# The first branch's output projection as seven products of split halves, with the gate weights in half rows beside it

## The chip, the cores and the metric

One core of one Trainium2 chip runs the whole kernel in one launch. The metric is device time in microseconds (us), as the median over executions.

## The reference

One decoder layer over 2048 tokens with 1024 channels, then a final RMSNorm:

```python
mod = c @ w_ada + b_ada                      # shift, scale, gate
h = rmsnorm(x) * (1 + scale) + shift
p = h @ w_in                                 # 8 column groups of 1024
a = val * sigmoid(glu)                       # branch A: causal depthwise conv, width 31
y_a = (silu(layernorm(conv(a))) * silu(za)) @ w_conv_out
y_b = (gelu(u) * mixing(layernorm(gelu(v))) * silu(zb)) @ w_sgu_out
merged = sigmoid(ga) * y_a + sigmoid(gb) * y_b
x = x + gate * (merged @ w_o);  out = rmsnorm(x, g_final)
```

Branch A is called the first branch here and its weights `w_a` (w_conv_out); branch B is the second, with `w_b` (w_sgu_out). `c` is one vector, so `gate` is one row of 1024 numbers, computed from 1024 x 1024 weights ("gate weights", `wgate`).

## The kernel before

**Stages.** The sequence is worked in two stages of 1024 tokens; a stage has two halves `h` of 512 tokens (T). Channels lie in 8 tiles of 128 partitions (KT = 8, half of it KH = 4). In each stage come, in this order: the v columns with the mixing; 28 groups of `w_in` columns ("quads"); the projection of the second branch (`std_pairs(yb, done_b)`); that of the first (`std_pairs(ya, done_a)`), with the merge in `done_a`; the output projection with `w_o` (`out_half(0)`, `out_half(1)`; in the last stage `finish_last` instead of the second).

**Numbers as two halves.** Each fp32 operand of a matmul is kept as a rounded part hi and a rest lo (`split`: ACT copies hi at L87, another engine subtracts at L88). `prod` multiplies weights by data over 4 channel tiles with three matmuls of 128x512 each (L329, L332, L335): 12 matmuls.

**Two ways to multiply.** A plain projection takes two column tiles and both halves h as four outputs, each of two `prod`s: 8 products. `quad` (L800 to 842) makes the same four outputs from 7 products on sums and differences of the operands (A11, A12, A22 are data tiles, S1 to S4 sums of them; the weight pieces are b11, b21, t1, t2, b22, t3, t4). Their outputs are combined on DVE: at L830 (`tt12` below) `c - p16` for output c12, at L834 (`tt22` below) `p5 - d` for output c22, where d is the PSUM bank into which the seventh product (A22) then goes on accumulating. That product is kept in `pending` and is issued in the next quad, behind its first product.

**Weights.** Every piece is prepared four `take()`s ahead: a 256 KB load into a `raw` tile (8 of them), then the split into a `whl` tile (5). For quads the sums and the lo parts are made on GpSimd (POOL); for plain projections lo is made on DVE.

**Order.** Background pieces wait in a list `bg`; `run_bg(n)` issues the next n after a product. A scheduler sets the final order on each engine; each engine then takes its own instructions strictly in order, and so does SP, which issues most DMAs. `load` (L76 to 79) brings a 128x512 tile of 256 KB by SP's queue into one of three buffers with the tag "ld": the names `gl` (gate values), `bl` (the second branch's products from DRAM), `zl`, `gb` in the profile are all such tiles, so a fourth load has to wait until one of the three is used. Other pools: 28 `hs` tiles (`yb`, `ya`, `mg`), 8 `x` tiles (`xn`, `wg`, `xo` of the last stage), 6 `t512` tiles, 6 PSUM banks.

**Around the change.** While the second branch's projection runs, `conv_out` in the background makes the 16 tiles `ya`. In the first branch's projection `done_a` multiplies a finished bank by `gl`, adds `bl` and splits the result into `mg`. In stage 0 `gate_step` multiplies eight rows of gate weights (512 KB each, loaded on POOL's queue) by the entries of c and adds them up in `acc` on DVE.

Of the kernel before, what the change touches and what calls it, by code (L numbers as in the profile page):

```python
# [7 lines left out]
F32 = mybir.dt.float32  # L8
# [3 lines left out]
ALU = mybir.AluOpType  # L12
# [28 lines left out]
def hybrid_layer(  # L41
# [203 lines left out]

    def quad_piece(q, kind):
        def prep():
            def r(kh, c):
                return part(w_in, q, kh, c)

# [21 lines left out]
            if kind == "t4":  # L272
                for kh in range(2):
                    for c in range(2):
                        raws.pop((id(w_in), q, kh, c))
            return w
# [5 lines left out]
    for s in range(NS):  # L282
        if s == 0:
            order += [make_row(w_v, d_wv, k, n) for n in range(2) for k in range(KT)]
        else:
            for _ in range(2):
                order += [load_row(d_wv, k, n) for n in range(2) for k in range(KT)]
        for q in range(NQ):
            order.append(quad_piece(q, "b11"))
            if q:  # L290
                order.append(quad_piece(q - 1, "t4"))
            order += [quad_piece(q, k) for k in ("b21", "t1", "t2", "b22", "t3")]
        order.append(quad_piece(NQ - 1, "t4"))
        for mat in (w_b, w_a):
            for q in range(4):
                order += [std_piece(mat, q, kh, c) for c in range(2) for kh in range(2)]
        for h in range(2):
# [426 lines left out]
    for s in range(NS):  # L724
# [68 lines left out]
        beside = [mix_second]  # L793
        A11, A12, A22 = A[0][:KH], A[0][KH:], A[1][KH:]

# [3 lines left out]

        def quad(c11, c12, c22, c21, in_psum):  # L800

            tt = nc.vector.tensor_tensor

# [9 lines left out]
            if pending:  # L813
                pending.pop()()
                run_bg(2)
            prod(a, [take()], A12, start=False)
            c11(a)
            run_bg(2)
            if beside:
                beside.pop()()  # L820
            c = bank()
            prod(c, [take()], S1)
            p5 = snap(c)
            run_bg(2)
            prod(d, [take()], S2, start=False)
# [136 lines left out]
        rdiag = [None, None]  # L962
        ya = [[None] * KT, [None] * KT]

# [86 lines left out]
        def std_pairs(rhs, done):  # L1051

# [17 lines left out]
        def load_xo(h, came=None):  # L1070
            xo = []
            for c in range(NC):
                o = xtile("xo")[:, :D] if last else hs32("xo")
                t0 = s * S + h * T + c * P
                if came is not None:
                    after(o[:, 0:1], came)
                (nc.gpsimd if last else nc.sync).dma_start(out=o, in_=x[t0 : t0 + P, :])
                xo.append(o)
            return xo


        if last:
            xos = [load_xo(h) for h in range(2)]
        if not last:
# [5 lines left out]
        if s == 0:  # L1090
            acc = []

            wg = []
            for r in range(KT):
                wg.append(xtile("wg")[:, :S])
                nc.gpsimd.dma_start(out=wg[r], in_=wgate[r * P : (r + 1) * P, :])

            def gate_step(r):
                if r == 0:
                    acc.append(row("acc"))  # L1100
                    nc.vector.tensor_scalar(
                        out=acc[0], in0=wg[0], scalar1=col(V_C, 0), scalar2=None, op0=ALU.mult
                    )
                else:
                    nc.vector.scalar_tensor_tensor(
                        out=acc[0], in0=wg[r], scalar=col(V_C, r), in1=acc[0],
                        op0=ALU.mult, op1=ALU.add,
                    )
# [12 lines left out]

        std_pairs(ya, done_a)
        run_bg(len(bg))


        came = mg[1][KT - 1][:, 1, 0:1].bitcast(F32)
        gate = hs32("gate")
# [24 lines left out]
        def out_half(h):  # L1152
            xo = xos[h] if last else load_xo(h, came)
            for n in range(2):
                pts = four(n)
# [60 lines left out]

        xn = [xtile("xn") for _ in range(KT)]
        for k in range(KT):
            after(xn[k][:, 0:1], acc[0][:, S - 1 : S])
        for h in range(2):  # L1220
            load_xn(s + 1, h, xn)
        A = [[], []]
        rxs = []

# [81 lines left out]
```

## Time and profile before

| what | value |
|---|---|
| median of 3 runs (lowest, highest) | 1863.58 us (1862.9, 1865.68) |
| the profiled execution | 1860.59 us |
| its span | 1858.9 us |
| granted TensorE clock in it | 0.998 of full |

A profile belongs to one execution: 1.69 us of its time lie outside its span, and it is 2.99 us shorter than the median. Times in the trace count from the start of the span. An arrow "out<-in" names the tile written and the one read; "x128" is a number of instructions. Engines are PE (matmul), DVE, ACT, POOL (GpSimd) and SP; a name with q is the queue or sequencer of an engine.

### The profile page before, as it was taken

The numbers are of one execution on the slowest core, as the hardware profiler recorded it, in microseconds if no ns is written. First come the engines' busy times: TensorE is split into PE (matmuls) and PEld (weight loads), VectorE is DVE, ScalarE is ACT, GpSimd is POOL, SyncE is SP. The second block draws the span as 40 slices with busy tenths as digits, with TensorE's granted clock in tenths as the row PEclk, the third lists the DMA queues.
The fourth block names the chain that finished last, engine by engine and source line by source line (L and its number), as shares of the span: only waits on it lengthen the run. The fifth ranks groups of instructions, "written<-read, shape, count | busy, mean of one in ns | idle before, by whom it ended". The sixth has DMA issues, their size and how long they took to land.

```text
span 1858.9 us, 23059 instructions
## 1 busy us (share of the span) xinstructions
PE 1823.4 (98%) x8096; PEld 1499.1 (81%) x8096; DVE 1318.9 (71%) x1569; ACT 854.9 (46%) x1392; POOL 895.0 (48%) x752
## 2 busy tenths in 40 slices
PE   6989999999999999999999999999999999999998
PEld 5778888888888787888888888888888887888886
DVE  7897789888889956455842687878978798534425
ACT  4835455555456751342612455555555457412112
POOL 0267767777777731001000777777777777110000
PEclk9999999999999999999999999999999999999999
DMA  9943233322333389768875332223323235964432
GB/s 374 373 156 127 76 120 108 113 98 71 111 108 113 114 326 315 252 202 289 318 282 193 132 119 93 86 100 107 114 97 99 83 134 172 348 227 149 133 145 91
DMA packets 136900, 309.97 MB, mean 167 GB/s; under 512 B 15664, under 2 KB 15664, under 8 KB 136784
## 3 DMA queue, kind: packets, MB, share of 16 engines
q1 hardware_dynamic: 101088, 219.20, 35.1%
q0 software_dynamic: 14384, 50.50, 7.1%
q10 hardware_dynamic: 21312, 38.81, 5.6%
q8 instruction: 63, 1.03, 0.2%
q14 instruction: 53, 0.43, 0.1%
HBM read 222.99 MB, written 85.46 MB: 166 GB/s over the span
## 4 chain that ended last, share of the span: by engine, by line
PE 86%; DMA 6%; DVE 4%; POOL 2%; issue 2%; ACT 1%; SPq 0%; DVEq 0%; POOLq 0%; ACTq 0%
PE bank L329 23%; PE bank L335 23%; PE bank L332 23%; PE bank L347 4%; PE bank L345 4%; PE bank L346 4%; PE bank L517 2%; PE cv L347 1%; PE cv L346 1%; PE cv L345 1%; POOL whl L88 1%; DMA zl<-sz 1%; DMA sx<-in_x 1%; DMA raw<-in_w_v 1%; DVE rsq L988 1%
## 5 line engine op out<-in xcount | busy, mean ns | idle before, releaser
L88 POOL TENSOR_TENSOR whl<-raw,whl 128x512 fp32r<-128x512 f32 x392 | 530.5, 1358 | 325.6 <-ACT whl L87 319.7
L858 DVE SCALAR_TENSOR_TENSOR cv<-a,vec,cv 128x1024 f32<-128x1024 f32 x464 | 597.0, 1287 | 31.5 <-ACT cv L852 21.4
L87 ACT ACTIVATE whl<-raw 128x512 fp32r<-128x512 f32 x488 | 305.6, 627 | 422.3 <-PE bank L335 246.0
L329 PE MATMUL bank<-s,whl 128*128 128x512 f32 x896 | 350.0, 391 | 0.0
L335 PE MATMUL bank<-s,whl 128*128 128x512 f32 x896 | 348.6, 389 | 0.0
L332 PE MATMUL bank<-s,whl 128*128 128x512 f32 x896 | 348.6, 389 | 0.0
L252 POOL TENSOR_TENSOR raw<-raw 128x512 f32<-128x512 f32 x224 | 296.1, 1322 | 17.3
L329 PE MATMUL bank<-h,whl 128*128 128x512 f32 x672 | 265.8, 395 | 4.7 <-ACT bank L811 4.7
L332 PE MATMUL bank<-h,whl 128*128 128x512 f32 x672 | 261.7, 389 | 0.0
L335 PE MATMUL bank<-h,whl 128*128 128x512 f32 x672 | 261.7, 389 | 0.0
L335 PEld LDWEIGHTS bank<-s,whl 128*128 128x128 f32 x896 | 168.2, 188 | 35.1
L332 PEld LDWEIGHTS bank<-s,whl 128*128 128x128 f32 x896 | 168.2, 188 | 35.1 <-issue 0.5
L329 PEld LDWEIGHTS bank<-s,whl 128*128 128x128 f32 x896 | 168.2, 188 | 35.1 <-issue 0.5
L329 PEld LDWEIGHTS bank<-h,whl 128*128 128x128 f32 x672 | 126.1, 188 | 38.2 <-ACT bank L811 6.4
L335 PEld LDWEIGHTS bank<-h,whl 128*128 128x128 f32 x672 | 126.1, 188 | 26.7
L332 PEld LDWEIGHTS bank<-h,whl 128*128 128x128 f32 x672 | 126.2, 188 | 26.4 <-issue 1.0
L806 ACT ACTIVATE snap<-bank 128x512 f32<-128x512 f32 x112 | 66.4, 597 | 88.4 <-PE bank L335 88.2
L335 PE MATMUL bank<-yb,whl 128*128 128x512 f32 x256 | 99.8, 390 | 2.1 <-DVE whl L88 2.1
L1175 POOL DMA_DIRECT2D out<-xo x12 | 6.4, 534 | 197.6 <-DVE xo L1171 197.6
L329 PE MATMUL bank<-yb,whl 128*128 128x512 f32 x256 | 99.6, 389 | 0.0
L332 PE MATMUL bank<-yb,whl 128*128 128x512 f32 x256 | 99.6, 389 | 0.0
L335 PE MATMUL bank<-ya,whl 128*128 128x512 f32 x256 | 99.6, 389 | 0.0
(234 smaller groups left out, 2844.7 us busy)
## 6 DMA issues: line engine op xcount, KB each, us to landing
raw<-in_w_in SPq DMA_DIRECT2D x224, 256.0 KB, 3.0
yb<-yb SPq DMA_DIRECT2D x32, 512.0 KB, 7.6
whl<-d_wv SPq DMA_DIRECT2D x32, 512.0 KB, 4.3
whl<-d_wo SPq DMA_DIRECT2D x21, 512.0 KB, 5.2
wa<-in_wada SPq DMA_DIRECT2D x16, 512.0 KB, 8.0
xn<-in_xt SPq DMA_DIRECT2D x32, 256.0 KB, 6.6
raw<-in_w_v SPq DMA_DIRECT2D x32, 256.0 KB, 7.4
d_wv<-whl POOLq DMA_DIRECT2D x16, 512.0 KB, 7.7
```

The lines of the kernel that those rows point to most:

```text
L87: nc.scalar.activation(hi, val, AF.Copy)
L88: eng.tensor_tensor(out=lo, in0=val, in1=hi.bitcast(F32), op=ALU.subtract)
L252: eng.tensor_tensor(out=dst, in0=dst, in1=src, op=ALU.add)
L329: nc.tensor.matmul(pt, wh, h[:, 0], start=start and k == 0, stop=False, skip_group_check=True)
L332: nc.tensor.matmul(pt, wh, h[:, 1], start=False, stop=False, skip_group_check=True)
L335: nc.tensor.matmul(pt, wl, h[:, 0], start=False, stop=k == last, skip_group_check=True)
L345: nc.tensor.matmul(pt, xh, wh, start=kt == 0, stop=False)
L346: nc.tensor.matmul(pt, xh, wl, start=False, stop=False)
L347: nc.tensor.matmul(pt, xl, wh, start=False, stop=kt == KT - 1)
L517: nc.tensor.matmul(pq[:, c * P : (c + 1) * P], vn[c][:, j * P : (j + 1) * P], wsT[:, j * P : (j + 1) * P], start=c == 0, stop=True, skip_g ...
L806: nc.scalar.activation(t, pt, AF.Copy)
L858: nc.vector.scalar_tensor_tensor(out=dst, in0=a[:, k : k + S], scalar=col(V_CW, j * TAPS + k), in1=cv[0], op0=ALU.mult, op1=ALU.add,)
```

## The change

1. `w_a` is prepared by `quad_piece` (28 pieces a stage, instead of 16 plain ones), and the first branch's projection is four `quad`s on `ya_ops`; the first of them does the S1 product ahead of A12 (`lead`).
2. Of `ya`, 12 of the 16 tiles are split; 16 sums `sy` of the unsplit `y` tiles are made in the background behind `conv_out`, and split into `hs` tiles.
3. `done_a` leaves the merged values unsplit in `m`, which takes the 8 `x` tiles; `merged` splits them later, six of the first half in the background of the last quad, the others behind it.
4. The gate weights come as 16 half rows of 256 KB through `load`, that is by SP's queue and the three "ld" buffers, and `gate_step` stands at every second place of the background list.
5. The loads `xn` for the next stage, which were issued before `out_half(0)`, are issued in its background. In the last stage `xo` is loaded after the merges, in half rows, its second half in the background of `out_half(0)`; `came` is a small tile of its own.

```diff
-    def quad_piece(q, kind):
+    def quad_piece(mat, q, kind):
...
-        for mat in (w_b, w_a):
-            for q in range(4):
-                order += [std_piece(mat, q, kh, c) for c in range(2) for kh in range(2)]
+        for mat, nq in ((w_in, NQ), (w_a, KH)):
+            if mat is w_a:
+                for q in range(4):
+                    order += [std_piece(w_b, q, kh, c) for c in range(2) for kh in range(2)]
+            for q in range(nq):
+                order.append(quad_piece(mat, q, "b11"))
+                if q:
+                    order.append(quad_piece(mat, q - 1, "t4"))
+                second = ("t1", "b21") if mat is w_a and q == 0 else ("b21", "t1")
+                order += [quad_piece(mat, q, k) for k in second + ("t2", "b22", "t3")]
+            order.append(quad_piece(mat, nq - 1, "t4"))
...
-            ya[h][j] = hs("ya")
-            split(ya[h][j], v)
+            if h == 0 or j >= KH:
+                ya.append(hs("ya"))
+                split(ya[-1], v)
...
+        sy = []
+        for f in (sum1, sum2, sum4, sum3):
+            bg.extend(lambda f=f, k=k: sy.append(f(y, k)) for k in range(KH))
...
-            wg = []
-            for r in range(KT):
-                wg.append(xtile("wg")[:, :S])
-                nc.gpsimd.dma_start(out=wg[r], in_=wgate[r * P : (r + 1) * P, :])
-
-            def gate_step(r):
+            def gate_step(r, n):
+                ns = slice(n * T, (n + 1) * T)
+                if not acc:
+                    acc.append(row("acc"))
+                wg = load(wgate[r * P : (r + 1) * P, ns], "wg")
...
-            for r in range(KT):
-                bg.insert(8 + 4 * r, lambda r=r: gate_step(r))
+            for i in range(2 * KT):
+                bg.insert(2 * i + 1, lambda i=i: gate_step(i // 2, i % 2))
...
-        def done_a(j, h, pt):
-            g, m = load(d_sa[j][h], "gl"), t512("m")
-            b = load(d_mb[j][h], "bl")
-            nc.vector.tensor_tensor(out=m, in0=pt, in1=g, op=ALU.mult)
-            nc.vector.tensor_tensor(out=m, in0=m, in1=b, op=ALU.add)
+        m = [None] * KT
+
+        def merged(h, j):
             mg[h][j] = hs("mg")
-            split(mg[h][j], m)
-
-        std_pairs(ya, done_a)
+            split(mg[h][j], m[j][:, h * T : (h + 1) * T])
+
+        def done_a(j, h):
+            def fin(pt):
+                if m[j] is None:
+                    m[j] = xtile("m")
+                v = m[j][:, h * T : (h + 1) * T]
+                g, b = load(d_sa[j][h], "gl"), load(d_mb[j][h], "bl")
+                nc.vector.tensor_tensor(out=v, in0=pt, in1=g, op=ALU.mult)
+                nc.vector.tensor_tensor(out=v, in0=v, in1=b, op=ALU.add)
+
+            return fin
+
+        for q in range(KH):
+            if q == KH - 1:
+                bg.extend(lambda j=j: merged(0, j) for j in range(KT - 2))
+            quad(
+                done_a(2 * q, 0), done_a(2 * q + 1, 0), done_a(2 * q + 1, 1),
+                done_a(2 * q, 1), True, ya_ops, q == 0,
+            )
         run_bg(len(bg))
+        for j in range(KT - 2, KT):
+            merged(0, j)
+        pending.pop()()
+        for j in range(KT):
+            merged(1, j)
...
+        pause(8)
+        bg.append(next_xn)
```

**The order at DVE, start of the first branch's projection, stage 0.** First before: L1117 is the multiplication by `gl`, L1118 the addition of `bl`, L88 a split.

```order
L1117 TENSOR_TENSOR m_6386<-bank_6359,gl_6384 128x512
L1118 TENSOR_TENSOR m_6386<-m_6386,bl_6387 128x512
L88 TENSOR_TENSOR mg_6391<-m_6386,mg_6391 128x512
L1117 TENSOR_TENSOR m_6428<-bank_6401,gl_6426 128x512
L1118 TENSOR_TENSOR m_6428<-m_6428,bl_6429 128x512
L88 TENSOR_TENSOR mg_6433<-m_6428,mg_6433 128x512
L88 TENSOR_TENSOR whl_6344<-raw_6345,whl_6344 128x512
```

Now the same place in the changed kernel: L1125 and L1130 are steps of the gate weights (`wg`), L1150 and L1151 the multiplication by `gl` and the addition of `bl`, L839 is `tt12` and L843 `tt22` of the first quad.

```order
L1130 SCALAR_TENSOR_TENSOR acc_6397<-wg_6451,vec_75,acc_6397 128x512
L1130 SCALAR_TENSOR_TENSOR acc_6397<-wg_6473,vec_75,acc_6397 128x512
L1150 TENSOR_TENSOR m_6442<-bank_6377,gl_6443 128x512
L1151 TENSOR_TENSOR m_6442<-m_6442,bl_6445 128x512
L1130 SCALAR_TENSOR_TENSOR acc_6397<-wg_6503,vec_75,acc_6397 128x512
L839 TENSOR_TENSOR bank_6401<-bank_6401,snap_6470 128x512
L1150 TENSOR_TENSOR m_6494<-bank_6401,gl_6495 128x512
L1151 TENSOR_TENSOR m_6494<-m_6494,bl_6497 128x512
L843 TENSOR_TENSOR snap_6418<-snap_6418,bank_6378 128x512
L1150 TENSOR_TENSOR m_6494<-snap_6418,gl_6525 128x512
L1151 TENSOR_TENSOR m_6494<-m_6494,bl_6527 128x512
```

Three steps of the gate weights stand among the first merge operations here (the rows for `wg_6398` and `wg_6422` stand ahead of these, among the `sy` splits), and `tt22`, which the seventh product needs, stands behind two additions of `bl`; the splits into `mg` are gone from here.

**The order at SP, same stretch.** Before, the issues are those of `gl`, `bl` and raw weights:

```order
L176 DMA raw_6530<-in_w_a 128x512
L78 DMA bl_6387<-mb00_187 128x512
L176 DMA raw_6535<-in_w_a 128x512
L176 DMA raw_6540<-in_w_a 128x512
L78 DMA gl_6426<-sa10_141 128x512
L176 DMA raw_6710<-in_w_a 128x512
L78 DMA bl_6429<-mb10_189 128x512
L78 DMA gl_6467<-sa01_140 128x512
```

In the changed kernel the half rows `wg` stand between them:

```order
L78 DMA wg_6398<-in_wgate 128x512
L78 DMA wg_6422<-in_wgate 128x512
L78 DMA gl_6443<-sa00_139 128x512
L78 DMA bl_6445<-mb00_187 128x512
L176 DMA raw_6615<-in_w_a 128x512
L78 DMA wg_6451<-in_wgate 128x512
L176 DMA raw_6661<-in_w_a 128x512
L78 DMA wg_6473<-in_wgate 128x512
L176 DMA raw_6690<-in_w_a 128x512
L78 DMA gl_6495<-sa10_141 128x512
L78 DMA bl_6497<-mb10_189 128x512
L176 DMA raw_6722<-in_w_a 128x512
```

Of these twelve issues eight go through the three "ld" buffers (`wg`, `gl`, `bl`), and each of them waits until a buffer is used up.

**The order at DVE, the second quad, stage 0, changed kernel.** The rows run from its first steps to its `tt22` (the last row); before, DVE had there the multiplications, additions and splits of the merge, and splits of weights.

```order
L1150 TENSOR_TENSOR m_6602<-bank_6535,gl_6603 128x512
L1151 TENSOR_TENSOR m_6602<-m_6602,bl_6605 128x512
L1130 SCALAR_TENSOR_TENSOR acc_6397<-wg_6611,vec_75,acc_6397 128x512
L1130 SCALAR_TENSOR_TENSOR acc_6397<-wg_6635,vec_75,acc_6397 128x512
L1130 SCALAR_TENSOR_TENSOR acc_6397<-wg_6658,vec_75,acc_6397 128x512
L839 TENSOR_TENSOR bank_6614<-bank_6614,snap_6654 128x512
L1130 SCALAR_TENSOR_TENSOR acc_6397<-wg_6687,vec_75,acc_6397 128x512
L1150 TENSOR_TENSOR m_6679<-bank_6614,gl_6680 128x512
L1151 TENSOR_TENSOR m_6679<-m_6679,bl_6682 128x512
L408 TENSOR_TENSOR rsn0_6817<-ss2_6375 128x4
L843 TENSOR_TENSOR snap_6632<-snap_6632,bank_6536 128x512
```

Four steps of the gate weights stand between the second quad's first merge and its `tt22` here, and one more pair of `gl` and `bl`.

## Rows read from the trace of the kernel before

**Rows 1.** The page: span, and the engines' busy time.

```profile
span 1858.9 us, 23059 instructions
...
PE 1823.4 (98%) x8096; PEld 1499.1 (81%) x8096; DVE 1318.9 (71%) x1569; ACT 854.9 (46%) x1392; POOL 895.0 (48%) x752
```

**Rows 2.** The page: the chain that ended last, by engine.

```profile
PE 86%; DMA 6%; DVE 4%; POOL 2%; issue 2%; ACT 1%; SPq 0%; DVEq 0%; POOLq 0%; ACTq 0%
```

**Rows 3.** Windows: start and end, length, busy time by engine, clock, DMA share.

```profile
core 0: us, PE busy (x) PEld busy (x) DVE busy (x) ACT busy (x) POOL busy (x), PEclk, DMA share, GB/s
675.00:768.00 93.00, 90.93 (x399) 74.44 (x398) 48.48 (x76) 21.30 (x35) 12.44 (x23) 1.00 0.90 316
768.00:855.00 87.00, 87.00 (x386) 72.06 (x385) 42.41 (x66) 31.85 (x66) 2.69 (x5) 1.00 0.64 208
855.00:942.00 87.00, 87.00 (x378) 70.65 (x377) 63.45 (x109) 34.70 (x56) 9.06 (x17) 1.00 0.89 330
1130.00:1520.00 390.00, 390.00 (x1716) 321.28 (x1716) 329.77 (x310) 210.04 (x329) 294.67 (x226) 1.00 0.30 102
1677.00:1764.00 87.00, 87.00 (x386) 72.06 (x385) 39.68 (x58) 17.09 (x27) 0.55 (x1) 1.00 0.44 138
```

**Rows 4.** Line L329 on PE, stage 0: ns shortest/median/longest, first and last start.

```profile
L329 PE MATMUL bank<-ya,whl x128: 389/389/389, 767.8 to 854.2; 128*128 128x512 f32 x128
```

**Rows 5.** Waits of PE, 660 to 1030 us: total us, times, longest.

```profile
PE bank L335 <- DVE whl L88: 2.1, 2, 1.1
```

**Rows 6.** The chain in order of time, 699 to 708: start, length, what.

```profile
700.94 0.70 DVE a L1045
...
701.66 3.24 DMA gl<-sbg
...
704.93 0.70 DVE mb L1064
```

**Rows 7.** DMA issues, 690 to 735: KB each, median us from issue to landing.

```profile
wg<-in_wgate POOLq DMA_DIRECT2D x8, 512.0 KB, 6.6
zl<-sz SPq DMA_DIRECT2D x9, 256.0 KB, 5.1
gl<-sbg SPq DMA_DIRECT2D x9, 256.0 KB, 4.2
```

**Rows 8.** DMA issues, 768 to 855, the first branch's projection of stage 0.

```profile
xs<-in_x ACTq DMA_DIRECT2D x16, 256.0 KB, 3.7
gl<-sa SPq DMA_DIRECT2D x15, 256.0 KB, 3.9
bl<-mb SPq DMA_DIRECT2D x15, 256.0 KB, 2.8
...
raw<-in_w_a SPq DMA_DIRECT2D x4, 256.0 KB, 4.0
```

**Rows 9.** DMA issues, 855 to 942, the output projection of stage 0.

```profile
xo<-in_x SPq DMA_DIRECT2D x8, 512.0 KB, 5.9
...
raw<-in_w_o SPq DMA_DIRECT2D x4, 256.0 KB, 14.6
```

**Rows 10.** DMA issues, 1677 to 1764, the first branch's projection of stage 1.

```profile
gl<-sa SPq DMA_DIRECT2D x15, 256.0 KB, 2.8
bl<-mb SPq DMA_DIRECT2D x15, 256.0 KB, 2.6
```

**Rows 11.** Groups of DVE by shape: busy us, mean ns; idle before.

```profile
L988 DVE TENSOR_TENSOR rsq<-rsq,q 128x512 f32<-128x512 f32 x28 | 33.6, 1206 | 2.1 <-ACT q L987 1.4
L1118 DVE TENSOR_TENSOR m<-m,bl 128x512 f32<-128x512 f32 x32 | 22.1, 689 | 1.1 <-DMA bl<-mb 0.5
L1105 DVE SCALAR_TENSOR_TENSOR acc<-wg,vec,acc 128x1024 f32<-128x1024 f32 x7 | 9.0, 1280 | 2.3 <-DMA wg<-in_wgate 2.3
```

**Rows 12.** GpSimd in quads, 200 to 600: ns shortest/median/longest, first and last start.

```profile
L88 POOL TENSOR_TENSOR whl<-raw,whl x147: 1281/1295/1309, 199.7 to 598.4; 128x512 fp32r<-128x512 f32 x147
...
L252 POOL TENSOR_TENSOR raw<-raw x84: 1287/1294/1305, 201.1 to 595.9; 128x512 f32<-128x512 f32 x84
```

More of the change, by code (lines that the diff above doesn't have):

```diff
@@ L244, in std_piece @@
         return prep
-    def quad_piece(q, kind):
+    def quad_piece(mat, q, kind):
         def prep():
             def r(kh, c):
-                return part(w_in, q, kh, c)
+                return part(mat, q, kh, c)
             def add(dst, src, eng):
@@ L274, in prep @@
                     for c in range(2):
-                        raws.pop((id(w_in), q, kh, c))
+                        raws.pop((id(mat), q, kh, c))
             return w
@@ L793, in hybrid_layer, with quad @@
         beside = [mix_second]
-        A11, A12, A22 = A[0][:KH], A[0][KH:], A[1][KH:]
+        ops = (A[0][:KH], A[0][KH:], A[1][KH:], S1, S2, S4, S3)
         pending = []
-        def quad(c11, c12, c22, c21, in_psum):
+        def quad(c11, c12, c22, c21, in_psum, ops=ops, lead=False):
+            A11, A12, A22, S1, S2, S4, S3 = ops
             tt = nc.vector.tensor_tensor
@@ L815, in quad @@
                 run_bg(2)
+            if lead:
+                c = bank()
+                prod(c, [take()], S1)
+                p5 = snap(c)
+                run_bg(2)
             prod(a, [take()], A12, start=False)
@@ L820, in quad @@
                 beside.pop()()
[L821 to L824, printed above, removed]
+            if not lead:
+                c = bank()
+                prod(c, [take()], S1)
+                p5 = snap(c)
+                run_bg(2)
             prod(d, [take()], S2, start=False)
@@ L962, in hybrid_layer @@
         rdiag = [None, None]
-        ya = [[None] * KT, [None] * KT]
         def half(h):
@@ L1076, in load_xo, with sy_group @@
                     after(o[:, 0:1], came)
-                (nc.gpsimd if last else nc.sync).dma_start(out=o, in_=x[t0 : t0 + P, :])
+                if last:
+                    nc.gpsimd.dma_start(out=o[:, :T], in_=x[t0 : t0 + P, :T])
+                else:
+                    nc.sync.dma_start(out=o, in_=x[t0 : t0 + P, :])
                 xo.append(o)
-            return xo
-        if last:
-            xos = [load_xo(h) for h in range(2)]
+            if last:
+                for c in range(NC):
+                    t0 = s * S + h * T + c * P
+                    nc.gpsimd.dma_start(out=xo[c][:, T:], in_=x[t0 : t0 + P, T:])
+            return xo
+        def sy_group(i):
+            group = []
+            for k in range(KH):
+                group.append(hs("sy"))
+                split(group[k], sy[i * KH + k])
+            return group
+        ya_ops = (ya[:KH], ya[KH:KT], ya[KT:], *(sy_group(i) for i in range(4)))
         if not last:
@@ L1105, in gate_step @@
                     nc.vector.scalar_tensor_tensor(
[L1106 removed]
+                        out=acc[0][:, ns], in0=wg, scalar=col(V_C, r), in1=acc[0][:, ns],
                         op0=ALU.mult, op1=ALU.add,
                     )
[L1110 to L1111 removed]
+            for i in range(2 * KT):
+                bg.insert(2 * i + 1, lambda i=i: gate_step(i // 2, i % 2))
         mg = [[None] * KT, [None] * KT]
[L1114 to L1126 removed]
+        m = [None] * KT
+        def merged(h, j):
+            mg[h][j] = hs("mg")
+            split(mg[h][j], m[j][:, h * T : (h + 1) * T])
[15 more added lines that the diff above has]
+            )
+        run_bg(len(bg))
+        for j in range(KT - 2, KT):
[3 more added lines that the diff above has]
+            merged(1, j)
+        if last:
+            xos = [load_xo(0)]
+        came = const.tile([P, 1], F32, name=f"came{s}")
+        after(came, m[KT - 2][:, T : T + 1])
         gate = hs32("gate")
@@ L1153, in out_half @@
             xo = xos[h] if last else load_xo(h, came)
+            if last:
+                bg.append(lambda: xos.append(load_xo(1)))
             for n in range(2):
@@ L1215, in hybrid_layer, with next_xn @@
             break
[L1217 to L1221, printed above, removed]
-        A = [[], []]
+        xn = []
+        A = [[], []]
+        def next_xn():
+            xn.extend(xtile("xn") for _ in range(KT))
+            for h in range(2):
+                load_xn(s + 1, h, xn)
+        pause(8)
+        bg.append(next_xn)
         rxs = []
```

11 lines of the change are left out of this document (3 added, 8 removed).

## The prediction, made before the changed kernel ran

> **What bounds the kernel now.** I read the page first. PE is busy for 98% of the span [rows 1], and the chain that ended last runs over PE for 86%, over DMA for 6% and DVE for 4% [rows 2]. That is an average over stages, so the windows come next, one for each stretch that the change touches. In the first branch's projection PE is busy for the whole window in both stages, 87.00 of 87.00 us, at full clock; DVE has 42.41 and 39.68 us of work there, POOL 2.69 and 0.55 [rows 3]. So this stretch is as long as its matmuls, in either stage, and fewer matmuls make it shorter as far as nothing else becomes late. In the second branch's projection of stage 0 (675 to 768) PE is busy for 90.93 of 93.00 us, and what it waits for is DVE's splits of weights, 2.1 us [rows 3, 5]. DMA stands at a share of 0.90 there, at 0.64 in the stretch behind it, at 0.89 in the output projection, and in stage 1 at 0.44 [rows 3]: transfers are crowded in stage 0 alone. This decides what may eat the gain.
>
> **What is removed from PE.** L329 starts 128 times in a stage, between 767.8 and 854.2 us [rows 4], and every start stands for three matmuls: (854.2 − 767.8) / 127 / 3 = 0.2268 us for a matmul. A product of 12 takes 2.72 us. Before, a stage had 4 groups of 8 products, 384 matmuls; now it has 4 quads of 7, 336. So 96 matmuls go, 48 in each stage: 96 × 0.2268 = **−21.8 us**. The order of instructions on PE shows the same 96.
>
> **What GpSimd takes over.** A stage now has 28 lo splits of `w_a` and 16 sums of raw tiles on POOL, at 1.295 and 1.294 us [rows 12]: 57 us in a stretch of 28 × 2.72 = 76 us. In the long stretch of `w_in` quads POOL is busy 294.67 of 390 us, the same 75%, and PE 390.00 of 390.00 [rows 3]. So I price it at nothing; the cover is that each piece is prepared four products ahead (10.9 us against two GpSimd operations of 1.3). DVE loses 16 splits of 0.69 in a stage and gains 16 sums and 16 splits of `sy`; it had more than half of its time free [rows 3].
>
> **The 2.1 us of waits on DVE.** DVE's long additions for the gate weights, 1.28 us each [rows 11], leave the second branch's projection; the splits for which PE waited [rows 5] stand in the same queue. Between nothing and 2.1 us come back; I take half, **−1.0**.
>
> **The gate weights' new place.** This is where I expect a loss. Before, eight loads of 512 KB came into tiles of their own. Now 16 half rows go through the three "ld" buffers, between `gl` and `bl`, and DVE works strictly in order. So a half row that has not landed holds up the merge behind it, and the merge frees the buffer for the next load. One round is: landing time L from issue, 0.03 until DVE starts, 0.70 of work, 0.02 until SP issues again (701.66 + 3.24 to 704.93, and 700.94 + 0.70 to 701.66 [rows 6]); L + 0.74 in all.
>
> I follow the rounds in the order of DVE's rows and of SP's. Time 0 is the start of the first product of the first quad. The last two groups of the second branch take 2 × 5.44 us, so the bank for `mb_6264` is ready at −10.9, and with a split and the multiplication behind it (0.7 each) its buffer is free at −9.5. From there ten rounds lie one behind another up to the second quad's `tt22`, those of wg_6398, wg_6422, wg_6451, wg_6473, wg_6503, bl_6527, gl_6576, gl_6603, wg_6635 and wg_6687. Each takes a buffer that the use of the one before it, or the operation just behind that use, sets free. Between them stands work in the same queue: five `sy` splits and a multiplication (3.6), two merge operations (1.3), `tt12` and a multiplication (1.3), one more step of the gate weights (0.6), and at the end two merge operations, a small one and `tt22` itself (2.1); together 8.9. So `tt22` is done at −9.5 + 8.9 + 10 × (L + 0.74) = 6.8 + 10 L.
>
> GpSimd adds to it. A DVE operation that reads two SBUF tiles took 0.69 us where POOL was idle, but 1.21 in the `rsq` group, which runs beside the quads [rows 11]. Nine operations on the chain are of this kind: 0 to 9 × 0.52 = 4.7 us, since POOL is busy three quarters of the time and not at every one; I take the middle, 2.3. That gives 9.1 + 10 L.
>
> PE needs this `tt22` before it may write the second quad's seventh product, because that accumulates into the bank d that `tt22` reads. That product is the 15th in PE's order (six of the first quad, seven of the second, one of the third, counting the first quad's seventh among the second's), so it is due at 14 × 2.72 = 38.1 us. Nothing is lost up to L = 2.9; beyond that each 0.1 us of L costs 1.0. The third quad has four such rounds in its 7 × 2.72 = 19.05 us, and falls behind only from L = 4.0 on.
>
> What is L? The trace of before has no half rows. The nearest are the 256 KB loads of the same stretch: `gl` 3.9, `bl` 2.8, `xs` 3.7, raw `w_a` 4.0 [rows 8], mean 3.6. From below: 2.6 to 2.8 in stage 1 [rows 10]; from above: `zl` 5.1 and `gl` 4.2 from 690 to 735 [rows 7]. I take 3.6, since the stretch keeps its transfers and gets 4 MB more, in a time that is a little shorter, but the eight 512 KB loads leave the stretch ahead of it. The loss is 9.1 + 36.0 − 38.1 = **+7.0 us**. In stage 1 there are no half rows, and two loads for each merge at 2.6 to 2.8 [rows 10]: nothing.
>
> Here the Trainium skill would have it otherwise, in the page "DMA: Bandwidth & Descriptors", section "Anatomy of one DMA — SWDGE (gpsimd) path": one transfer takes about 2.0 us plus its bytes over 436,000, which is an estimate of 2.6 us for 256 KB. The rows of stage 1 agree with it, those of stage 0 (2.8 to 4.0) do not [rows 8, 10]; by it no product would wait and the sum would come out near 1842.
>
> **The rest.** `wg` leaves the `x` tiles, so the merged values can lie there; 336 matmuls need no other bank than the quads before had. The `mg` splits behind the last quad lie beside PE's seventh product and the first products of the output projection (tiles of the first half are split in the background): nothing, at most 1.4 us for two splits that come too late. In the output projection of stage 0 eight loads `xn` of 256 KB now go to SP ahead of `xo` and of the last four raw tiles of `w_o`. DMA is at 0.89 there; these raw tiles landed after 14.6 us [rows 9]. 2 MB at 330 GB/s [rows 3] are 6.4 us. PE can use the raw tiles as they come four pieces ahead, so 0 to 5 of that reach it; I take **+1.5**, nearer to nothing because the preparation ahead covers most. In the last stage the `xo` loads move behind the merges, where DMA stands at 0.44: nothing.
>
> **Sum.** 1860.59 − 21.8 − 1.0 + 7.0 + 1.5 = 1846.3 for an execution like the profiled one. The median of the runs is 2.99 us above that one; on this footing 1849.3.
>
> **The rivals.**
> (B) The half rows are hidden: L is 2.9 or less, because the eight large loads no longer crowd the stretch ahead. For it: stage 1's rows; against it: every load of stage 0 but `bl`. Time: 1849.3 − 7.0 = 1842.3. Chance 0.22.
> (C) The other side, one mechanism: the same chain with late landings, at L = 5.0 as `zl` had at 306 to 316 GB/s [rows 3, 7]. The second quad then waits 9.1 + 50.0 − 38.1 = 21.0 us, and the third 4 × (5.0 + 0.74 + 0.26) − 19.05 = 5.0 more. That makes 26.0 in place of 7.0: 1868.3, slower than before. Loss outweighs gain by 3.7 us from L = 4.9 on; from 4.4 to 4.9 the time is within 0.2% of before. For it: four more MB in a stretch at a share of 0.64; against it: `gl` there took 3.9 with the same three buffers. Chance 0.08 for the slower, 0.10 for the middle.
> (D) GpSimd blocks DVE for longer. If each of the nine operations met a fresh one of POOL and waited it out, it would cost 9 × 1.30 = 11.7 in place of 2.3: 1858.7. Against it: `rsq` lost 0.52 on the mean, not 1.30 [rows 11]. Chance 0.05.
> The Trainium skill bears on this with the page "SBUF — State Buffer", section "SBUF: two separate sides": it calls the pair of ports that these two engines share an exclusive lock, whose loser waits for the whole instruction; by it (D) is what the worst order does.
> (E) The output projection pays in full for the `xn` loads, +5 in place of +1.5: 1852.8. Chance 0.05. The change does what it says (the 96 matmuls are gone from PE's order), so no chance stands for the opposite.
>
> **How the numbers follow.** My forecast has 0.50. With (B), (D) and (E) "faster" would have 0.82, (C) gives 0.10 to "same" and 0.08 to "slower". 0.2% is 3.7 us, about what a measurement of this kernel can tell from no change: faster is below 1859.9, slower above 1867.3. As mishaps that I have not seen can only be on that side, I move 0.02 from "faster". The range goes down to (B) with all of the 2.1 us and nothing in the output projection, 1849.3 − 7.0 − 1.1 − 1.5 = 1839.7, and up to L = 4.4, about 1861; outside lie most of (C) and little else.
>
> **What would show it.** PE has 96 matmuls fewer at the same pitch. In stage 1 the stretch is 76 us plus what the last product adds, without waits: 10.9 us shorter. In stage 0 PE waits before the seventh product of the second quad, on DVE's `tt22`, for about 7 us, with DVE idle on `wg` loads of about 3.6 us; no such wait speaks for (B), waits in the third and fourth quads for (C). DVE's additions there at 0.7 to 1.0 us; at 2.0, (D) holds. PE's waits on `whl` splits in the second branch's projection fall to about 1 us. I would be wrong above all if SP's queue delays raw weights of `w_a` behind loads that wait for a buffer, so that PE waits on `whl` and not on `tt22`.

## The result, and the profile after

| kernel | median, us | lowest to highest | runs |
|---|---|---|---|
| before | 1862.9 | 1861.09 to 1865.68 | 5 |
| after | 1869.57 | 1867.89 to 1873.57 | 5 |

The ratio of after to before is 1.0051, 95% interval 1.0040 to 1.0061: the change makes the kernel slower, where the prediction had it faster. The profiled execution of after took 1873.57 us, the longest of its five and 4.0 above their median; what follows is read from that execution.

The page of the changed kernel (span 1871.9 us): busy time by engine, and the chain that ended last by engine.

```profile
PE 1817.0 (97%) x8000; PEld 1488.6 (80%) x8000; DVE 1369.9 (73%) x1611; ACT 891.8 (48%) x1464; POOL 1014.6 (54%) x840
...
PE 83%; DVE 6%; DMA 5%; issue 2%; ACT 2%; POOL 2%; SPq 0%; DVEq 0%; POOLq 0%; ACTq 0%
```

The 96 matmuls are gone, but PE is busy for only 6.4 us less than before [rows 1], where 21.8 were due: some of its time is spent at a lower clock (granted 0.989 of full on the mean, before 0.998). DVE's share of the chain has grown from 4% to 6% [rows 2].

Where the time went shows in the first starts of the matmuls. For both kernels, the line of `prod`'s first matmul (ns shortest/median/longest, first and last start): the second block is the kernel before.

```profile
L331 PE MATMUL bank<-yb,whl x128: 388/389/389, 676.2 to 765.5; 128*128 128x512 f32 x128
...
L331 PE MATMUL bank<-ya,whl x48: 389/389/796, 766.2 to 862.1; 128*128 128x512 f32 x48
L331 PE MATMUL bank<-h,whl x336: 389/389/798, 1055.4 to 1605.9; 128*128 128x512 f32 x168
...
L331 PE MATMUL bank<-ya,whl x48: 389/389/496, 1692.7 to 1770.8; 128*128 128x512 f32 x48
L347 PE MATMUL bank<-whl,mg x136: 388/389/1354, 863.2 to 1856.1; 128*128 128x512 f32 x136
L347 PE MATMUL bank<-wo,mg x72: 389/389/793, 1784.2 to 1863.6; 128*128 128x512 f32 x72
```

```profile
L329 PE MATMUL bank<-yb,whl x128: 388/389/402, 675.2 to 767.2; 128*128 128x512 f32 x128
L329 PE MATMUL bank<-h,whl x336: 389/389/793, 1039.7 to 1590.3; 128*128 128x512 f32 x168
L329 PE MATMUL bank<-ya,whl x128: 389/389/389, 1677.1 to 1763.5; 128*128 128x512 f32 x128
L345 PE MATMUL bank<-whl,mg x136: 387/389/799, 856.2 to 1843.0; 128*128 128x512 f32 x136
L345 PE MATMUL bank<-wo,mg x72: 389/389/389, 1777.8 to 1850.5; 128*128 128x512 f32 x72
```

With [rows 4] for the start of the first branch before, these starts cut the span into stretches. The names A, O and E are used below; "forecast" is before plus the prediction's terms.

| stretch | before | forecast | after |
|---|---|---|---|
| second branch, stage 0 (first start `yb` to `ya`) | 92.6 | 91.6 | 90.0 |
| A: first branch, stage 0 (`ya` to `mg`) | 88.4 | 84.5 | 97.0 |
| O: output of stage 0 to the first quad of stage 1 (`mg` to `h`) | 183.5 | 185.0 | 192.2 |
| E: first branch and output of stage 1 (`ya` to last `wo`) | 173.4 | 162.5 | 170.9 |

Forecast and measurement are 12.5, 7.2 and 8.4 us apart in A, O and E, and −1.6 in the second branch; 1.0 us came in ahead of all of these. In each of the three PE waits, where before it waited in none.

PE's waits in A and O (the first block) and in E (the second): total, times, longest.

```profile
PE bank L331 <- DVE snap L843: 12.2, 3, 8.4
PE cv L348 <- DVE whl L88: 2.4, 2, 2.1
PE cv L347 <- ACT whl L87: 1.3, 1, 1.3
PE bank L331 <- ACT snap L809: 1.2, 1, 1.2
PE bank L347 <- DVE m L1150: 1.1, 1, 1.1
PE bank L347 <- DMA whl<-d_wo: 0.5, 1, 0.5
```

```profile
PE bank L347 <- DMA wo<-d_wo: 3.7, 1, 3.7
PE bank L331 <- ACT snap L809: 1.2, 1, 1.2
```

**Stretch A.** L843 is `tt22`, as forecast, but the long wait is that of the first quad. DVE's timeline shows why (start, length, engine, line, operation; in brackets the idle time before it and what ended it; x7 is a run of seven):

```profile
756.09 0.68 DVE L1077 TENSOR_TENSOR mb<-bank,gl 128x512 f32<-128x512 f32 x1
...
763.83 5.29 DVE L88 TENSOR_TENSOR sy<-a,sy 128x512 fp32r<-128x512 f32 x5
...
769.64 5.30 DVE L88 TENSOR_TENSOR sy<-a,sy 128x512 fp32r<-128x512 f32 x2
774.87 1.78 DVE L1130 SCALAR_TENSOR_TENSOR acc<-wg,vec,acc 128x512 f32<-128x512 f32 x1
780.00 0.85 DVE L1130 SCALAR_TENSOR_TENSOR acc<-wg,vec,acc 128x512 f32<-128x512 f32 x1 [3.36 <-DMA wg<-in_wgate]
...
788.36 1.85 DVE L1130 SCALAR_TENSOR_TENSOR acc<-wg,vec,acc 128x512 f32<-128x512 f32 x1 [6.18 <-DMA wg<-in_wgate]
...
793.03 0.68 DVE L843 TENSOR_TENSOR snap<-snap,bank 128x512 f32<-128x512 f32 x1
```

The chain starts as worked out: `mb_6264` ends at 756.8, 9.4 us before the first quad. Then seven `sy` splits take 10.6 us (the last two 0.68 and 4.70), three gate steps up to 1.85, and two rounds wait 3.4 and 6.2 us for their half row. `tt22` ends at 793.7, and PE, whose seventh product was due at 785.2, starts it at 793.76. PE's timeline there:

```profile
784.99 0.39 PE L337 MATMUL bank<-ya,whl 128*128 128x512 f32 x1
793.76 0.80 PE L331 MATMUL bank<-ya,whl 128*128 128x512 f32 x1 [8.38 <-DVE snap L843]
794.36 0.63 PE L334 MATMUL bank<-ya,whl 128*128 128x512 f32 x1
```

After the wait the matmuls start 0.43 us apart instead of 0.23: from 794.0 to 799.4 us the granted clock is 0.50 of full, the lower of its two levels. The second quad's wait, and matmuls behind it:

```profile
819.08 0.50 PE L331 MATMUL bank<-ya,whl 128*128 128x512 f32 x1 [3.24 <-DVE snap L843]
...
820.50 0.63 PE L337 MATMUL bank<-ya,whl 128*128 128x512 f32 x1
820.93 0.63 PE L331 MATMUL bank<-ya,whl 128*128 128x512 f32 x1
```

Groups of DVE by shape in 766 to 864 (busy us, mean ns, idle before):

```profile
L1130 DVE SCALAR_TENSOR_TENSOR acc<-wg,vec,acc 128x512 f32<-128x512 f32 x14 | 15.9, 1145 | 22.5 <-DMA wg<-in_wgate 22.5
L1151 DVE TENSOR_TENSOR m<-m,bl 128x512 f32<-128x512 f32 x14 | 15.0, 1072 | 5.1 <-DMA bl<-mb 4.7
L88 DVE TENSOR_TENSOR sy<-a,sy 128x512 fp32r<-128x512 f32 x5 | 9.4, 1924 | 0.0
L1150 DVE TENSOR_TENSOR m<-bank,gl 128x512 f32<-128x512 f32 x11 | 7.5, 686 | 2.6 <-DMA gl<-sa 1.3 <-PE bank L337 1.2
```

The three groups here with two SBUF inputs are long, against 0.69 us for such an operation before [rows 11]; the one whose first input lies in PSUM takes 0.69 us. DVE idles 22.5 us for half rows.

**Stretch O.** Windows of the changed kernel (columns as in [rows 3]), and its DMA issues in 864 to 950:

```profile
864.00:884.00 20.00, 18.86 (x84) 15.28 (x83) 12.76 (x29) 3.46 (x6) 3.17 (x6) 1.00 0.93 305
884.00:904.00 20.00, 16.30 (x58) 10.90 (x57) 10.36 (x17) 5.17 (x9) 2.13 (x4) 0.91 1.03 413
```

```profile
xn<-in_xt SPq DMA_DIRECT2D x16, 256.0 KB, 6.1
...
raw<-in_w_o SPq DMA_DIRECT2D x4, 256.0 KB, 16.4
```

The DMA share is 1.03 from 884 to 904, and PE waits for pieces of the last raw tiles of `w_o` (L87, L88). These take 16.4 us, not much more than before [rows 9], but SP, behind `xn` and `xo`, issues them only 16.2 us after the start of the stretch, where before one came at once and three from 9.2 us on.

**Stretch E.** A window, and the issues of 1760 to 1800:

```profile
1790.00:1800.00 10.00, 9.23 (x29) 7.41 (x30) 2.90 (x5) 0.00 (x0) 0.00 (x0) 0.68 1.03 413
```

```profile
wo<-d_wo SPq DMA_DIRECT2D x10, 512.0 KB, 14.7
xo<-in_x POOLq DMA_DIRECT2D x16, 256.0 KB, 9.0
```

The 4 MB of `xo`, all issued at once behind the merges, run against the `w_o` tiles; after a wait of 3.7 us PE works at a granted clock of 0.68 in this window.

### The profile page after: what moved, and what is told of

The parts are those of the page before. It is cut to its first block, busy times and chain, and to the rows that moved or that the text cites. A ratio compares the mean times of both kernels' runs of the same rounds, so it can differ in the third digit from the quotient of the medians.

```text
span 1871.9 us, 23178 instructions
## 1 busy us (share of the span) xinstructions
PE 1817.0 (97%) x8000; PEld 1488.6 (80%) x8000; DVE 1369.9 (73%) x1611; ACT 891.8 (48%) x1464; POOL 1014.6 (54%) x840
## 4 chain that ended last, share of the span: by engine, by line
PE 83%; DVE 6%; DMA 5%; issue 2%; ACT 2%; POOL 2%; SPq 0%; DVEq 0%; POOLq 0%; ACTq 0%
PE bank L331 23%; PE bank L334 23%; PE bank L337 23%; PE bank L347 3%; PE bank L349 3%; PE bank L348 3%; PE bank L519 2%; POOL whl L88 1%; DMA wsT<-d_ws 1%; DVE wa L475 1%; PE cv L349 1%; PE cv L347 1%; PE cv L348 1%; DMA wg<-in_wgate 1%; DMA wo<-d_wo 1%
## 5 line engine op out<-in xcount | busy, mean ns | idle before, releaser
L88 POOL TENSOR_TENSOR whl<-raw,whl 128x512 fp32r<-128x512 f32 x448 | 605.5, 1357 | 380.8 <-ACT whl L87 377.6
L87 ACT ACTIVATE whl<-raw 128x512 fp32r<-128x512 f32 x512 | 320.5, 627 | 430.6 <-PE bank L337 231.3
L252 POOL TENSOR_TENSOR raw<-raw 128x512 f32<-128x512 f32 x256 | 342.7, 1339 | 19.7
L809 ACT ACTIVATE snap<-bank 128x512 f32<-128x512 f32 x128 | 75.7, 596 | 106.8 <-PE bank L337 106.6
L1078 POOL DMA_DIRECT2D mb<-mb x32 | 17.5, 546 | 147.0 <-DVE mb L1077 137.2
L903 DVE TENSOR_TENSOR a<-bank,snap 128x512 f32<-128x512 f32 x16 | 11.1, 692 | 85.8 <-ACT bank L902 85.8
```

The source lines that it names most:

```text
L87: nc.scalar.activation(hi, val, AF.Copy)
L88: eng.tensor_tensor(out=lo, in0=val, in1=hi.bitcast(F32), op=ALU.subtract)
L252: eng.tensor_tensor(out=dst, in0=dst, in1=src, op=ALU.add)
L809: nc.scalar.activation(t, pt, AF.Copy)
```

## Experiments

Each was timed beside the kernel before. The letters are the stretches; the kernel after had 97.0, 192.2, 170.9.

| run | median / before | ratio (95%) | A | O | E |
|---|---|---|---|---|---|
| e1_gate_back | 1863.43 / 1859.97 | 1.0015 (1.0006, 1.0024) | 90.7 | 192.3 | 169.1 |
| e2_xn_late | 1873.57 / 1859.97 | 1.0072 (1.0059, 1.0085) | 96.4 | 196.4 | 172.1 |
| e3_xo_late | 1865.67 / 1859.97 | 1.0028 (1.0019, 1.0037) | 94.9 | 191.9 | 164.4 |
| e4_all_three | 1862.25 / 1859.97 | 1.0007 (0.9998, 1.0016) | 90.6 | 196.3 | 165.1 |
| e5_one_sbuf_input | 1869.66 / 1859.71 | 1.0046 (1.0032, 1.0059) | 93.8 | 193.1 | 169.1 |
| e6_no_gate_rounds | 1855.19 / 1859.71 | 0.9969 (0.9959, 0.9980) | 80.2 | 192.6 | 171.1 |
| e7_w_o_twice | 1862.56 / 1859.71 | 1.0015 (1.0006, 1.0024) | 95.8 | 183.4 | 170.0 |
| e8_all_repairs | 1854.95 / 1859.71 | 0.9970 (0.9960, 0.9981) | 94.7 | 184.1 | 165.4 |
| e9_gate_early | 1854.34 / 1861.1 | 0.9959 (0.9946, 0.9971) | 79.2 | 191.6 | 169.9 |
| e10_gate_early_and_repairs | 1840.19 / 1861.1 | 0.9884 (0.9870, 0.9899) | 79.3 | 183.4 | 164.8 |
| e11_before_w_o_twice | 1861.71 / 1861.1 | 1.0001 (0.9992, 1.0010) | | | |

**e1, the gate weights as before.**

```diff
-            def gate_step(r, n):
...
+                wg.append(xtile("wg")[:, :S])
+                nc.gpsimd.dma_start(out=wg[r], in_=wgate[r * P : (r + 1) * P, :])
...
+                bg.insert(8 + 4 * r, lambda r=r: gate_step(r))
```

> The changed kernel with the gate weights as before: eight loads of 512 KB on POOL's queue into x tiles, eight long steps on DVE, all else of the change kept. Theory (half rows in the load chain make the second branch of waits): PE's 12.2 us of waits on tt22 in stage 0 and the low clock behind them (about 4 us) go, some 2 us of waits on weight splits come back; the median falls by about 15, to 1855. Rival (the chain is late because GpSimd holds up DVE's two-input operations, the gate steps are only some of them): the sy splits and the bl additions stay long, half of the wait stays; about 1863. Rival (PE would wait for something else as soon as this is gone): 1868 to 1870.

By the ratios about half of the gain expected (1.0051 to 1.0015), 6.3 us in A. The wait on `tt22` is gone, but this is not the old state: the `x` tiles are held by the convolution's outputs until the `sy` splits have read them, so the loads start at 763 only and the long steps fall beside GpSimd's work. DVE and POOL in this kernel, 765 to 857:

```profile
L1131 DVE SCALAR_TENSOR_TENSOR acc<-wg,vec,acc 128x1024 f32<-128x1024 f32 x7 | 15.6, 2227 | 1.7 <-DMA wg<-in_wgate 1.6
```

```profile
L252 POOL TENSOR_TENSOR raw<-raw 128x512 f32<-128x512 f32 x13 | 21.8, 1679 | 0.9
```

A step takes 2.23 us against 1.28 [rows 11], a sum on GpSimd 1.68 against 1.29 [rows 12]. PE now waits for ACT, three times and 8.8 us in all: 3.7 where ACT stands behind a late load `xs`, 2.4 where it stands behind such a sum, 2.7 where it stands behind an addition of `bl`. So the first rival's time came true (1863), and its long additions (1.13 us on the mean), but not its wait on `tt22`.

**e2, xn late.**

```diff
+            for k in range(KT):
+                after(xn[k][:, 0:1], late)
...
-        pause(8)
-        bg.append(next_xn)
+        pause(32)
...
+                if not last and h == 0 and n == 0:
+                    next_xn(xo[0][:, 0:1])
```

> The changed kernel with the next stage's xn loads made to wait for the first residual of out_half(0), so that they are issued behind xo and the last four raw tiles of w_o. Theory (the xn loads ahead of these raw tiles make PE wait in the output projection of stage 0): its 5.2 us of waits and the low clock behind them go; the output projection gets 7 to 8 us shorter, median about 1862. Rival (the stretch has too many bytes in any order, DMA share 1.0): the waits move to another tile of the same stretch, 1867 to 1871.

The rival held in kind, and the kernel was slower than it said: PE's waits for pieces of raw `w_o` in O are replaced by one of 8.1 us, on the reloads of split `w_o` for `out_half(1)`, which now stand behind the `xn` loads on SP.

```profile
PE bank L347 <- DMA whl<-d_wo: 8.1, 1, 8.1
```

The raw tiles of `w_o` still took 15.9 us, with one `xn` load ahead of them instead of eight; issued 14.1 us into the stretch instead of 16.2, they no longer hold up PE. So this other order at SP moves the wait and does not remove it.

**e3, xo late; e4, the three together.**

```diff
+        def xo_part(xo, h, c, n, w):
+            ns = slice(n * T, (n + 1) * T)
+            t0 = s * S + h * T + c * P
+            after(xo[c][:, n * T : n * T + 1], parts(w)[0][:, 0:1].bitcast(F32))
+            nc.gpsimd.dma_start(out=xo[c][:, ns], in_=x[t0 : t0 + P, ns])
...
+                    if last and n == 0 and 2 <= kt < 6:
+                        xo_part(xo, 0, kt - 2, 0, w)
```

> The changed kernel with the last stage's xo loads tied to the arrival of w_o tiles: half row c of the first half behind tile 2 + c, the others behind tiles 8 to 15. Theory (4 MB of xo on POOL's queue collide with the w_o tiles on SP's): the 3.7 us wait on wo and the low clock behind it (about 3 us) go; median about 1863. Rival (xo comes too late then): DVE's residuals wait for xo, the banks come free late and PE waits there instead, 1868 or more.

> The edits of the three other runs of this call together: gate weights as before, xn late, xo late. Theory (three separate losses, which add): 1869.6 - 15 - 7.5 - 6.5 = about 1841, close to 21.8 us below the kernel before. Rival (the losses are not separate, or the GpSimd work is the cause): 1850 or more.

e3 takes 6.5 us off E and the wait on `wo` away. PE's waits in its E:

```profile
PE bank L331 <- ACT snap L809: 1.2, 1, 1.2
```

E still misses its forecast by 1.9 us, and these 1.2 are in that. e4 has e1's A, e2's O and e3's E: the effects add, two of the three repairs were poor. Its rival's number (1850 or more) came true, its reasons did not.

**e5, one SBUF input.**

```diff
-                    acc.append(row("acc"))
+                    acc.append(wide())
...
-                nc.vector.tensor_tensor(out=v, in0=pt, in1=g, op=ALU.mult)
-                nc.vector.tensor_tensor(out=v, in0=v, in1=b, op=ALU.add)
+                nc.vector.tensor_tensor(out=pt, in0=pt, in1=g, op=ALU.mult)
+                nc.vector.tensor_tensor(out=v, in0=pt, in1=b, op=ALU.add)
```

> The changed kernel with the same loads, the same steps in the same order on DVE and the same work on GpSimd; but acc lies in PSUM (the wide tile, copied to SBUF at the end) and the merge multiplies in place in the PSUM bank, so that a gate step and, where the product is still in PSUM, the addition of bl read one SBUF tile and not two. Theory (GpSimd holds up DVE operations with two SBUF inputs, and through the rounds this makes tt22 late): the gate steps go from 1.15 us to about 0.75, these additions from 1.07 to 0.69, GpSimd's operations come back toward 1.30; PE's waits on tt22 in stage 0 fall from 12.2 to 3 to 6, the stretch from 96.8 to about 89, the median by 6 to 9. Rival (the landings alone make the chain): the durations may fall, but the waits stay at 10 or more, median 1 to 3 lower.

DVE in 762 to 857, and PE's waits on `tt22`:

```profile
L1130 DVE SCALAR_TENSOR_TENSOR cv<-wg,vec,cv 128x512 f32<-128x512 f32 x14 | 10.5, 751 | 19.6 <-DMA wg<-in_wgate 19.6
L88 DVE TENSOR_TENSOR sy<-a,sy 128x512 fp32r<-128x512 f32 x6 | 10.0, 1720 | 0.0
...
L1151 DVE TENSOR_TENSOR m<-bank,bl 128x512 f32<-128x512 f32 x11 | 7.6, 692 | 7.7 <-DMA bl<-mb 7.5
```

```profile
PE bank L331 <- DVE snap L843: 8.7, 3, 5.4
```

With loads, order and GpSimd's work unchanged, the gate steps go from 1.15 to 0.75 us and these additions from 1.07 to 0.69: sharing with GpSimd made them long, the `sy` splits still are. But PE's waits on `tt22` stay between the theory (3 to 6) and the rival (10 or more), A gets only 3.2 us shorter, and the median no lower that the runs could tell. The effect is real and small; the chain of landings stays.

**e6, no rounds of half rows.**

```diff
-            for i in range(2 * KT):
+            for i in range(2):
                 bg.insert(2 * i + 1, lambda i=i: gate_step(i // 2, i % 2))
```

> The changed kernel with 14 of the 16 half rows of gate weights left out, loads and steps; the two steps of the first row stay (the gate is computed from one row of weights only). Theory (the rounds of half rows in the chain, lengthened by GpSimd): no wait on tt22 is left in stage 0, the first branch's stretch takes 80 to 82 us instead of 96.8; median about 14 to 16 below the changed kernel, 1855 where before is 1860. Rival (GpSimd's work for the quads is too slow by itself): PE waits for weight pieces or for ACT behind them, the stretch stays at 87 or more.

A takes 80.2 us, 16.8 less, and no wait on `tt22` is left. PE's waits there:

```profile
PE bank L331 <- ACT snap L809: 1.8, 2, 1.2
```

So the rounds are the loss of A, and GpSimd's work for the quads is no bound. This kernel leaves most of the gate out; e9 below has all of it.

**e7, w_o made twice.**

```diff
-                order += [make_row(w_o, d_wo, k, n) for n in range(2) for k in range(KT)]
+                order += [make_row(w_o, None, k, n) for n in range(2) for k in range(KT)]
             elif s == 0:
-                order += [load_row(d_wo, k, n) for n in range(2) for k in range(KT)]
+                order += [make_row(w_o, d_wo, k, n) for n in range(2) for k in range(KT)]
```

> The changed kernel with other traffic in the output projection of stage 0: out_half(0) writes no split w_o to DRAM (8 MB less), out_half(1) makes its pieces again from raw w_o (4 MB of loads for 8 MB) and writes them. The xn loads stay where the change puts them. Theory (too many bytes in the first half of this stretch since the 4 MB of xn came into it): the raw w_o tiles land sooner than 10 us, the waits of 5.2 us there and the low clock go, from the first product of w_o to the first quad of stage 1 it takes 184 to 186 us instead of 192.2; median 6 to 8 lower. Rival (it is the order on SP, xn ahead of the last four raw tiles): they still come late, 190 or more.

O is back at 183.4 us, with `xn` still ahead on SP, and PE has no wait there. Windows of this kernel, the same places in O as above:

```profile
859.00:879.00 20.00, 20.00 (x88) 16.19 (x88) 13.48 (x30) 5.71 (x11) 0.56 (x1) 1.00 0.91 327
879.00:899.00 20.00, 20.00 (x86) 15.88 (x85) 15.13 (x25) 10.59 (x18) 0.53 (x1) 1.00 0.75 265
```

The loss of O is one of bytes: DMA falls from 1.03 to 0.75 in the second window, and the four raw tiles of `w_o` behind `xo` are issued 10.3 us into the stretch and land after 9.4 to 10.5 us.

**e8, the repairs of e3, e5 and e7 together.**

> The edits of the two runs with PSUM operands and with w_o made twice, and the late xo loads of an earlier run, together. Theory (three places, and the losses add): 7.5 + 7 + 6.5 below the changed kernel, about 12 to 15 us below the kernel before, 1846 where before is 1860. Rival (one repair's traffic or waits take up what another gives, as with the late xn loads): 1855 or more.

14 us less by the stretches of O and E, but A keeps the rounds; the expectation had credited e5 with more than it gave, and the time is at the rival's 1855.

**e9, the gate weights in the second branch's projection; e10, with the repairs of e3 and e7; e11, e7's edit alone in the kernel before.**

```diff
-                wg = load(wgate[r * P : (r + 1) * P, ns], "wg")
+                wg = wp.tile([P, T], F32, tag="raw", name="wg", bufs=8)
+                nc.sync.dma_start(out=wg, in_=wgate[r * P : (r + 1) * P, ns])
```

The whole block stands ahead of `std_pairs(yb, done_b)`, and `acc` in PSUM as in e5.

> The changed kernel with the 16 half rows moved to the second branch's projection of stage 0: loaded into raw tiles (eight buffers) instead of the three ld buffers, with acc in PSUM, so that the first branch's projection has none of them and nothing is left out. Theory (the rounds of half rows are the whole loss of that stretch): the first branch's stretch takes 80 to 82 us as without the half rows, PE does not wait on tt22; the second branch's stretch stays at 90 to 92 us; median 14 to 17 below the changed kernel, about 1854 to 1856 where before is 1860. Rival (the loss moves with them): the second branch's stretch grows by 5 or more, through waits on weight splits behind gate steps.

> The same with w_o made twice in stage 0 and the late xo loads. Theory (three losses of about 16.6, 9 and 6 us by the traces, in three places): 21 to 24 us below the kernel before, 1836 to 1840 where before is 1860. Rival (they interact, as the late xn loads did): 1845 or more.

> The kernel before with w_o made twice in stage 0, nothing else. It has no wait of PE in that stretch, so the theory says no change, 0 to 1 us either way, and what the repaired kernel gains is the change's own; the rival is that less traffic helps by itself, 3 us or more.

e9 computes everything and has A at 79.2; the second branch's stretch stays at 90.0 (673.9 to 763.9). e10 is 1.2% faster than before, 20.9 us by the medians, just under what was expected. e11 shows that `w_o` made twice gives the old kernel nothing: it only removes what the change had added. The other edits of e10 were not tried in the old kernel. Windows of e9, second and first branch of stage 0, and the longest of PE's waits in e10 from 660 to 1840:

```profile
673.00:763.00 90.00, 90.00 (x398) 74.28 (x397) 63.18 (x98) 28.30 (x49) 16.89 (x22) 1.00 0.80 273
763.00:843.00 80.00, 78.78 (x344) 64.19 (x343) 49.68 (x59) 43.95 (x93) 55.48 (x43) 1.00 0.72 228
```

```profile
PE bank L331 <- ACT snap L809: 2.4, 2, 1.2
...
```

## Why the prediction was wrong

Three terms were too small, each at a place of its own: the half rows (+7.0 in A, by the runs 17.8 with the clock behind the waits), `xn` (+1.5 in O, 8.7) and `xo` (nothing in E, 6.5). The gain was a little smaller too.

**The matmuls: right, but not what stands behind them.** 96 are gone, at 0.2268 us each. A without rounds takes 79.2 to 80.2 us, 28 products of 2.72 and some 3 us more, where before had 1.3 us beside its 32. So in e10 A and E are 9.1 and 8.6 us shorter, not 10.9 each: 17.7 of the 21.8 us. Most of the rest of e10's 20.9 is the second branch. One part of the difference is known: in e10 PE waits 1.2 us in each stage for ACT's copy at L809, and this copy stands behind the first half of an `mg` split, which itself waits for an addition of `bl`. The `mg` splits were priced at nothing. GpSimd priced at nothing: right for its own work, since PE waits for no weight piece in e6; its price falls on DVE.

**The half rows: right mechanism, mis-sized, and the long wait at another place.** The forecast was `tt22` of the second quad at 45.1 us after the first product; it ended at 819.0 − 766.2 = 52.8. Landing was right: 3.4 us for the half rows, 3.3 for `gl`, 3.8 for `bl` (medians), for L = 3.6. The Trainium skill (page "DMA: Bandwidth & Descriptors", section "Anatomy of one DMA — SWDGE (gpsimd) path") gives 2.0 us plus the bytes over 436,000 for a DMA that GpSimd issues, by estimate 2.6 us here; these loads are SP's, and all three medians lie above it.

Three items make up the 7.7 us; together they are about 8.5, and rounds that landed sooner than 3.6 took some back. (1) Sharing with GpSimd in gate steps and additions: 2.3 was taken; in e5, without it, the same `tt22` ends at 811.3 − 762.9 = 48.4, so it is 4.4 between these two executions, close to the bound of 4.7. (2) The `sy` splits, priced at 0.69 though they too read two SBUF tiles: the first five took 5.29 instead of 3.0. The last two, which the sum leaves out because DVE would have to wait for `wg_6451` there anyway, took 5.30, longer than that landing; some 4 us together. (3) One half row that landed 6.0 us after its issue (782.38 to 788.36), not 3.6; why is open (in e5 the same one took 5.5).

Items 2 and 3 fall ahead of the first quad's `tt22`, which the prediction did not work out. By its own terms, without GpSimd's part, it would be done at −9.5 + 5 × 4.34 + 7.6 = 19.8 us, where PE needs it at 7 × 2.72 = 19.0. It was done at 27.5: the long wait of 8.4 us came there, and the second quad, where 7.0 was forecast, waited 3.2.

**The clock: a term that was missing.** I priced a wait at its length. Behind the waits of 8.4 and 3.2 us some 13 and 8 matmuls ran at 0.43 instead of 0.23 us, 4 us in A alone. The waits of 12.2 and this clock are 16.4 of the 17.8 us between A after and A in e9.

**`xn` in O: mis-sized, by a wrong step.** "Nearer to nothing because the preparation ahead covers most" took +1.5 between 0 and 5; it was 8.7. I looked at eight loads ahead of four raw tiles, that is at order and at 2 MB. But all 4 MB, which before were issued between 724.0 and 758.7 in the second branch's projection, move into a stretch whose DMA share was 0.89 [rows 3], because the merged values hold the `x` tiles. With fewer bytes and the same order the loss is gone (e7); with the same bytes and another order it is not (e2, the one other order tried).

**`xo` in E: "nothing" was wrong, it was about 6.5.** I read the cover from the window ahead of the merges (share 0.44), but the loads are issued behind them, against the `w_o` tiles, at 1.03.

**The second branch: right and more.** It got 2.6 us shorter, the bound was 2.1. In e9 sixteen short steps of the gate weights stand in this stretch again and it still takes 90.0 us, so it is not that steps stand there; whether it was their length, the splits of weights that went to GpSimd or the loads that left was not tried.

The rival on the other side (C) had the sign, not the reason: late landings were not needed. Three losses of known places came instead, of 17.8, 8.7 and 6.5 us, against gains of 9.2 in A (e9), 9.0 in E (e3) and 2.6 in the second branch. That makes 12.2 us; the two profiled executions are 13.0 apart, the medians 6.7.

The port that DVE and GpSimd share, which the Trainium skill calls an exclusive lock (page "SBUF — State Buffer", section "SBUF: two separate sides"), agrees with e5: with one input in PSUM the same operations are short again, and GpSimd's sums went from 1.54 to 1.34 us on the mean (in e6, which keeps the additions with two SBUF inputs, they took 1.58). The longest was one `sy` split of 4.70 us, from 770.2 on, beside three GpSimd operations that ran from 770.6 to 774.4 one behind another: more than the one operation that (D) had priced. An operation with a single SBUF input was not always spared: the first gate step took 0.85 us beside GpSimd, its other half 0.47 while GpSimd was idle.

## What to carry to other kernels

Where loads share a few buffers and an engine works in order, write the rounds down up to the first operation for which PE waits, and price every operation beside GpSimd by the number of its SBUF inputs; then add what the clock takes behind a wait. A load that "moves" takes its bytes along: compare the DMA share of the place where it is issued after the change, not that of the place where it stood. And undo each part alone before the change is judged: here a gain of 20 us lay under three losses, each with a repair of its own.

## What the runs showed of the hardware

After a wait of 8.4 us PE's first 13 matmuls ran at the lower of its two clock levels, 0.43 us apart (granted clock 0.50 from 794.0 to 799.4). Behind a wait of 3.2 us the first four ran at 0.23 us (granted clock 1.00 from 819.0 to 820.1), and the eight after them at 0.43 (0.50 from 820.2 to 823.4): there the clock fell only after PE had started again.
